# Six of the eight adaLN row tiles of a type, in the first norm's first half, loaded two at a time into the weights' hi and lo buffers

## The chip, the cores and the metric

The kernel runs on one core of a Trainium2 chip. The metric is the device time of one execution in microseconds, as the median over several runs; one execution was also taken with the hardware profiler. In what follows PE is TensorE's matmul side, PEld its weight loads, DVE is VectorE, ACT is ScalarE, POOL is GpSimd and SP is SyncE, which issues nearly all DMAs.

## The reference, cut to what matters

Two trunk layers of a diffusion backbone, in float32. Each sub-layer normalises its input and modulates it with a shift and a scale that come from a small vector `c` (for the 256 latent tokens) or `c_ctx` (for the 256 context tokens) through one large weight, `w_ada`. The change touches only the first such product of layer 0, so this is what must be seen:

```python
def rmsnorm(x, g):
    y = x * lax.rsqrt(jnp.mean(x * x, axis=-1, keepdims=True) + EPS)
    return y * g

def modulate(x, g, shift, scale):
    return rmsnorm(x, g) * (1 + scale) + shift

def adaln(v, w, b):                      # w: (1024, 6144)
    m = jax.nn.silu(v) @ w + b
    return jnp.split(m, 6, axis=-1)      # sh1, sc1, g1, sh2, sc2, g2

# layer l:
h  = modulate(x,  norm1[l], sh1, sc1)    # then h @ w_in and three token mixers, merge, MLP
hc = modulate(xc, norm1[l], csh1, csc1)
```

No column of the first norm's output can be formed before the shift and the scale of that column are there, and no matmul with `w_in` before that.

## The kernel before, in words

**Precision.** Every float32 product is made of three matmuls: an operand is split into a high part (ACT copies it to the rounded type `fp32r`) and a low part (DVE subtracts the high part from the operand). A weight tile of 128 x 1024 floats (512 KB) is loaded into a stage buffer `st` (4 buffers) and split into `wh` and `wl` (4 buffers each, `W_HL_BUFS`).

**The first norm's modulation.** Shift (type 0) and scale (type 1) of the first norm in layer 0 are computed as rows on PE. The 1024 columns of a type fall into two halves of 512 columns; for each half the class `First` accumulates, over the eight blocks `kk` of 128 rows of `w_ada`, a 4 x 512 product with the silu of `c` and `c_ctx` (two vectors, each with its hi and lo part). One block of one type and one half is a "row tile" of 128 x 512 floats, 256 KB. `ada_row` takes one of the 64 general buffers `b` for it and issues its load (`ad<-in_wada_dram` in the profile). `ada_use` splits it: ACT writes `ah` (a cast), DVE writes `al` (a subtraction), and `First.row` issues two matmuls (`ada<-ah,s` and `ada<-al,s`). After the eighth block `First.end` copies the 4 x 512 result out with ACT (`arow`), turns it into columns with matmuls (`adat`), and DVE adds the bias (`mod`); with both types there, DVE forms the factor `A`. Then ACT writes the first `hh`, the hi part of the normalised and modulated input, and the first matmul with `w_in` (`qkv<-wh,hh`) can start. The input itself comes in four tiles of 512 KB (`x` 0 and 1 latent, 2 and 3 context): ACT squares and sums them (`junk`), DVE and POOL make `rstd` (POOL's part is a power), DVE scales (`xh`), PE transposes (`xT`).

**What sets the order.** The list `START` gives the order of the first loads on SP's queue: tile (type 0, kk 0), `x` 0, `x` 1, the other 15 row tiles of half 0 with the types in turn, then the first weight tiles of `w_in` (`win`), `x` 2, one more `win`, the row tiles of half 1 with `x` 3 between them, and so on. Everything behind that, on every engine, is put in order while the program is written: each piece of work is a Python generator, and the scheduler `_Flow` runs the one of highest priority whose inputs are there by its own estimate of times (`fl.ready`, `fl.room` for buffers). A change of the estimated times early on can so change the written order later. `fl.room("w", ...)` is the count of `wh`/`wl` buffers in use, `fl.free` gives a buffer back.

```python
START = (
    [("ada", 0, 0, 0), ("x", 0), ("x", 1)]
    + [("ada", 0, typ, kk) for kk in range(KD) for typ in range(2)][1:]
    + [("win", 0, 0), ("win", 0, 1), ("x", 2), ("win", 0, 2)]
    + [("ada", 1, typ, kk) for kk in range(4) for typ in range(2)]
```

Of the kernel before, what the change touches and what calls it, by code (L numbers as in the profile page):

```python
# [8 lines left out]
F32 = mybir.dt.float32  # L9
F32R = mybir.dt.float32r  # L10
# [5 lines left out]
P = 128  # L16
D = 1024
KD = D // P
# [11 lines left out]
W_HL_BUFS = 4  # L30
# [30 lines left out]


START = (
    [("ada", 0, 0, 0), ("x", 0), ("x", 1)]
    + [("ada", 0, typ, kk) for kk in range(KD) for typ in range(2)][1:]
    + [("win", 0, 0), ("win", 0, 1), ("x", 2), ("win", 0, 2)]
    + [("ada", 1, typ, kk) for kk in range(4) for typ in range(2)]
    + [("x", 3)]
# [108 lines left out]
class _Flow:  # L177
# [58 lines left out]
    def free(self, *aps):  # L236

        for name in {ap.tensor.name for ap in aps}:
            self.shares[name] -= 1
            if self.shares[name]:  # L240
                continue
            p = self.pools[self.owner.pop(name)]
            p[0] -= 1
            p[1].append(self.uses[name] + 0.1)
# [48 lines left out]
P_NORM, P_ATT, P_SPLIT, P_SIDE, P_ADA, P_MAIN = range(6)  # L293
# [3 lines left out]
def kernel(ctx: ExitStack, tc: tile.TileContext, a: dict, out: bass.AP):  # L297
    nc = tc.nc
    ctx.enter_context(tc.manual_schedule())
    fl = _Flow()  # L300
# [6 lines left out]
    wp = ctx.enter_context(tc.tile_pool(name="wp", bufs=W_STAGE_BUFS))  # L307
# [6 lines left out]
    def nm(s):  # L314
        uid[0] += 1
        return f"{s}_{uid[0]}"

    def big(dt=F32, s="b"):
        t = bp.tile([P, 512], dt, tag="b", name=nm(s))
        fl.take("b", t)  # L320
        return t

    tmp = big
    free = fl.free
# [20 lines left out]
    def load(dst, src, queue=nc.sync):  # L345
        size = 4
        for d in dst.shape:
            size *= d
        fl.loaded(dst, size) if dst.space == bass.MemoryType.SB else None
        queue.dma_start(out=dst, in_=src)  # L350


    def stage(src, nk, ncol):

        yield from fl.room("st", 1, W_STAGE_BUFS)
        st = wp.tile([P, 1024], F32, tag="st", name=nm("st"))
        fl.take("st", st)
        v = st[:, : nk * ncol].rearrange("p (k n) -> p k n", k=nk)
        load(v, src)
        return v  # L360
# [8 lines left out]
    def halves(v, nk, ncol):  # L369

        yield fl.ready(v)
        yield from fl.room("w", 1, W_HL_BUFS)
        hi = wp.tile([P, 1024], F32R, tag="wh", name=nm("wh"), bufs=W_HL_BUFS)
        lo = wp.tile([P, 1024], F32R, tag="wl", name=nm("wl"), bufs=W_HL_BUFS)
        fl.take("w", hi)
        hv = hi[:, : nk * ncol].rearrange("p (k n) -> p k n", k=nk)
        lv = lo[:, : nk * ncol].rearrange("p (k n) -> p k n", k=nk)
        S.copy(out=hv, in_=v)
        yield fl.ready(hv)
        V.tensor_tensor(out=lv, in0=v, in1=hv.bitcast(F32), op=ALU.subtract)  # L380
        free(v)
        return hi, [(hv[:, k], lv[:, k]) for k in range(nk)]
# [56 lines left out]
    def mm3(ps, lh, rh, start, stop):  # L439

        PE.matmul(ps, lh[0], rh[0], start=start, stop=False)
        PE.matmul(ps, lh[0], rh[1], start=False, stop=False)
        PE.matmul(ps, lh[1], rh[0], start=False, stop=stop)
# [27 lines left out]
    x = [[None, None] for _ in range(NT)]  # L471
# [256 lines left out]
    def constants():  # L728
        load(rope, a["rope"])
        load(gains, a["gains"].to_broadcast([P, DEPTH, 4, HD]))  # L730
        load(sink, a["sink"].to_broadcast([P, DEPTH, NH]))
        load(icnt, a["icnt"])
        load(pscale, a["pscale"])
        fl.spawn(constants_use(), P_SIDE)
# [58 lines left out]
    def norm(l, which, stream, hT):  # L793
        xh = [[None, None, (_Event(), _Event())] for _ in range(2)]
        for i in range(2):
            fl.spawn(norm_tile(l, which, 2 * stream + i, xh[i]), P_NORM)
        first = (l, which) == (0, 0)
        if not first:
            yield ab_ev[l, which, stream][1]
        for k2 in range(0, KD, 2):  # L800
            for i in range(2):
                if late(xh[i][2][k2 // 4]):
                    yield xh[i][2][k2 // 4]
            if first and k2 == 4:
                yield ab_ev[l, which, stream][1]
            yield from banks()
            ps = bank("xT")
            for kk in range(2):
                k = k2 + kk
                for i in range(2):  # L810
                    c = (k % 4) * P
                    PE.transpose(ps[:, kk * 256 + i * P : kk * 256 + (i + 1) * P], xh[i][k // 4][:, c : c + P], ident)
            if k2 % 4 == 2:
                free(*[xh[i][k2 // 4] for i in range(2)])
            left = [0, 1]
            cols = slice(stream * 256, stream * 256 + 256)
            for kk in range(2):
                k = k2 + kk
                fl.spawn(mod_out(l, which, hT, stream, k, ps[:, kk * 256 : (kk + 1) * 256], cols, hT.ev[stream][k], H32_DVE.get((l, which, stream), ()), ps, left), P_NORM)
            yield  # L820
# [1166 lines left out]
    def main():  # L1987
        nxt = []

        def hT_next():  # L1990
            if not nxt:
                nxt.append(Normed())
            return nxt[0]

        yield from layer(0, h0, hT_next)
        yield from layer(1, nxt[0], None)
# [5 lines left out]
    def start():  # L2002

        def ada_row(half, typ, kk):
            yield from fl.room("b", 1, B_BUFS)
            raw = big(s="ad")
            load(raw, a["wada"][0, 2 * typ + half, kk // 4, :, kk % 4])
            fl.spawn(ada_use(first[half], typ, kk, raw), P_NORM)

        def ada_use(f, typ, kk, raw):  # L2010
            yield fl.ready(raw)
            yield from fl.room("b", 2, B_BUFS)
            hi, lo = big(F32R, "ah0"), big(F32R, "al0")
            S.copy(out=hi, in_=raw)
            yield fl.ready(hi)
            V.tensor_tensor(out=lo, in0=raw, in1=hi.bitcast(F32), op=ALU.subtract)
            free(raw)
            yield from f.row(typ, kk, (hi, lo))
            free(hi, lo)

        def x_rows(t):
            src = (a["x"] if t < 2 else a["ctx"])[0, t % 2 * P : t % 2 * P + P]
            v = yield from stage(src.unsqueeze(1), 1, D)
            for n in range(2):
                x[t][n] = v[:, 0, n * 512 : n * 512 + 512]
                fl.set(x_ev[t][n], v)
            if t % 2:
                fl.spawn(norm(0, 0, t // 2, h0), P_NORM)

        def win(kh, c):  # L2030
            if c < 2:
                k0, nk, ncol = 4 * kh + 2 * c, 2, 512
                src = a["win2"][0, 0]
            else:
                k0, nk, ncol = 4 * kh, 4, 256
                src = a["win"][0, CHUNKS[0][c]]
            v = yield from stage(src[:, k0 : k0 + nk], nk, ncol)
            fl.spawn(win_use(kh, c, v, nk, ncol), P_NORM)

        def win_use(kh, c, v, nk, ncol):  # L2040
            p, done = first_w[kh, c]
            p.extend((yield from halves(v, nk, ncol)))
            fl.set(done, *[q for r in p[1] for q in r])

        def mask_load():
            v = yield from stage(a["mask"], 2, P)
            fl.spawn(mask_use(v), P_NORM)

        def mask_use(v):
            yield fl.ready(v)  # L2050
            S.copy(out=mask, in_=v)
            free(v)

        first = [First(0), First(1)]
        fl.spawn(main(), P_MAIN)
        for it in START:
            if it[0] == "x":
                yield from x_rows(it[1])
            elif it[0] == "ada":
                yield from ada_row(*it[1:])  # L2060
            elif it[0] == "win":
                yield from win(*it[1:])
            elif it[0] == "const":
                constants()
            else:
                yield from mask_load()
        fl.spawn(ws.loads(), P_NORM)
        fl.spawn(ws.splits(), P_SPLIT)
        yield ab_ev[0, 0, 1][1]
        fl.set(layer_started[0])  # L2070

    plan_layer(0)
    plan_layer(1)
    fl.spawn(start(), P_NORM)
    fl.spawn(ada_all(), P_ADA)
    for l in range(DEPTH):
# [66 lines left out]
```

## Time and profile before

| | us |
|---|---|
| median of 3 runs | 1147.7 (1146.86 to 1148.02) |
| profiled execution, its own time | 1147.47 |
| its span, first to last instruction | 1145.7 |
| PE busy | 1123.3 (98%) |
| PEld busy | 946.2 (83%) |
| DVE busy | 890.5 (78%) |
| ACT busy | 646.9 (56%) |

The span is what the trace covers; 1.77 us of the profiled execution's own time lie outside it. A busy PE is not a PE at its peak, since matmuls are pipelined and their ends are modelled. DMA share is the mean busy share of the core's 16 DMA engines; for short stretches it can read a little over 1, because a packet counts where it begins.

### The profile page before, as it was taken

To read this page: it belongs to the slowest core of one execution; us is meant where nothing else is said; L and a number is where in the kernel's file an instruction comes from. 1 tells how busy PE (TensorE), PEld (TensorE's weight loads), DVE (VectorE), ACT (ScalarE), POOL (GpSimd) and SP (SyncE) were. 2 spreads that over 40 slices of the span, in tenths; PEclk is the share of its full clock that TensorE was granted. 3 is DMA by queue.
4 is the path that set the end of the run, shared out by engine and by line. 5 is a ranking of instruction groups with operands and counts; after the bars stand their busy time and mean duration, and the time that the engine had idled before them with its cause. 6 is when DMAs were issued, how large, how long until landed. Compare 5 with 4: busy or idle time off the path is not lost.

```text
span 1145.7 us, 16194 instructions
## 1 busy us (share of the span) xinstructions
PE 1123.3 (98%) x5760; PEld 946.2 (83%) x5760; DVE 890.5 (78%) x1681; ACT 646.9 (56%) x1372; POOL 64.2 (6%) x78
## 2 busy tenths in 40 slices
PE   6999999999999999999999999999999999999998
PEld 2788888888888898888888888889888888888886
DVE  6889888899899679888676734579777885999453
ACT  7867668657653574422133333576878864666432
POOL 1133002000000100000000000013010000000000
PEclk9999999999999999999999999999999999999999
DMA  9742332343554335455655533555325570776662
GB/s 333 268 151 92 119 124 80 114 163 120 166 170 158 123 120 195 155 194 174 200 202 187 200 112 106 171 166 176 104 69 171 178 264 1 247 261 209 191 213 75
DMA packets 59761, 186.74 MB, mean 163 GB/s; under 512 B 7040, under 2 KB 7824, under 8 KB 59680
## 3 DMA queue, kind: packets, MB, share of 16 engines
q1 hardware_dynamic: 59472, 185.63, 48.7%
q8 instruction: 45, 0.74, 0.3%
q14 instruction: 36, 0.29, 0.1%
q0 software_dynamic: 64, 0.07, 0.0%
q10 hardware_dynamic: 144, 0.01, 0.0%
HBM read 184.63 MB, written 1.05 MB: 162 GB/s over the span
## 4 chain that ended last, share of the span: by engine, by line
PE 89%; DVE 4%; ACT 4%; DMA 2%; issue 1%; SPq 0%; POOL 0%; DVEq 0%; ACTq 0%
PE tm L170 27%; PE h L170 22%; PE g L170 16%; PE qkv L170 6%; PE br L170 4%; PE po L170 2%; PE sc L170 2%; PE pT L174 2%; PE u L170 1%; DMA ad<-in_wada_dram 1%; ACT hh L136 1%; ACT p L136 1%; PE xT L174 1%; PE ada L170 1%; PE qT L174 1%
## 5 line engine op out<-in xcount | busy, mean ns | idle before, releaser
L136 DVE TENSOR_TENSOR wl<-st,wh 128x1024 fp32r<-128x1024 f32 x216 | 263.4, 1221 | 117.7 <-ACT wh L136 117.5
L136 ACT CAST wh<-st 128x1024 fp32r<-128x1024 f32 x216 | 227.9, 1059 | 224.2 <-PE tm L170 137.3
L170 PE MATMUL h<-hh,wh 128*128 128x512 f32 (+1 forms) x512 | 183.7, 378 | 0.0
L170 PE MATMUL h<-hh,wl 128*128 128x256 f32 (+1 forms) x512 | 168.2, 328 | 0.9 <-DVE wl L136 0.9
L136 DVE SCALAR_TENSOR_TENSOR acc<-sta,s_col,acc 128x512 f32<-128x512 f32 x224 | 159.3, 745 | 1.5 <-DMA sta<-in_wada_dram 1.1
L170 PE MATMUL tm<-wh,ah 128*128 128x512 f32 x384 | 149.9, 390 | 0.0
L170 PE MATMUL tm<-wl,ah 128*128 128x512 f32 x384 | 149.5, 389 | 0.0
L170 PE MATMUL tm<-wh,al 128*128 128x512 f32 x384 | 149.4, 389 | 0.0
L170 PEld LDWEIGHTS h<-hh,wh 128*128 128x128 f32 x512 | 96.2, 188 | 17.7
L170 PE MATMUL h<-hl,wh 128*128 128x512 f32 (+1 forms) x288 | 105.5, 366 | 0.1
L170 PEld LDWEIGHTS h<-hh,wl 128*128 128x128 f32 x512 | 96.6, 189 | 10.0 <-DVE wl L136 1.1
L170 PEld LDWEIGHTS tm<-wh,al 128*128 128x128 f32 x384 | 72.1, 188 | 15.2
L170 PEld LDWEIGHTS tm<-wl,ah 128*128 128x128 f32 x384 | 72.1, 188 | 14.9
L170 PEld LDWEIGHTS tm<-wh,ah 128*128 128x128 f32 x384 | 72.1, 188 | 14.6
L170 PE MATMUL g<-hh,wh 128*128 128x512 f32 x192 | 76.7, 400 | 0.0
L170 PE MATMUL g<-hh,wl 128*128 128x512 f32 x192 | 75.0, 391 | 0.0
L170 PE MATMUL g<-hl,wh 128*128 128x512 f32 x192 | 75.0, 391 | 0.0
L170 PE MATMUL qkv<-wh,hh 128*128 128x256 f32 (+1 forms) x192 | 66.1, 344 | 1.1 <-ACT hh L136 1.1
L170 PE MATMUL qkv<-wl,hh 128*128 128x256 f32 (+1 forms) x192 | 64.7, 337 | 1.8 <-DVE wl L136 1.8
L170 PE MATMUL qkv<-wh,hl 128*128 128x256 f32 (+1 forms) x192 | 64.8, 337 | 0.0
L170 PEld LDWEIGHTS h<-hl,wh 128*128 128x128 f32 x288 | 54.3, 189 | 9.2 <-DVE hl L136 0.5
L136 DVE TENSOR_REDUCE mx<-sc 128x1 f32<-128x512 f32 (+1 forms) x60 | 39.8, 685 | 20.8 <-PE sc L170 20.6
(213 smaller groups left out, 2238.0 us busy)
## 6 DMA issues: line engine op xcount, KB each, us to landing
st<-in_w_dram SPq DMA_DIRECT2D x136, 512.0 KB, 4.4
sta<-in_wada_dram SPq DMA_DIRECT2D x80, 512.0 KB, 4.1
st<-in_win_dram SPq DMA_DIRECT2D x48, 512.0 KB, 4.3
st<-in_wing_dram SPq DMA_DIRECT2D x24, 512.0 KB, 4.4
ad<-in_wada_dram SPq DMA_DIRECT2D x32, 256.0 KB, 6.7
st<-in_wout_dram SPq DMA_DIRECT2D x8, 512.0 KB, 4.5
wor<-in_wout_dram SPq DMA_DIRECT2D x16, 256.0 KB, 6.0
grow<-in_b_ada_dram SPq DMA_DIRECT2D x12, 256.0 KB, 5.5
```

Of the source, the lines that this page charges most:

```text
L136: return fn(*args, **kw)
L170: return self._e.matmul(out, lhsT, rhs, start=start, stop=stop)
L174: return self._e.transpose(out, in_, identity)
```

## The change

Blocks 0 to 5 of half 0 no longer come one row tile at a time. A new generator `ada_rows2(half, kk)` takes one pair of the `wh`/`wl` buffers and loads two consecutive blocks of type 0 into the first and the same two blocks of type 1 into the second: two loads of 512 KB in place of four of 256 KB. In `w_ada` as it lies in memory the two blocks of a row are next to each other, so that a partition's row is 4 KB long where it was 2 KB. Blocks 6 and 7 still come one by one. The uses are unchanged (`ada_use` for each of the four 512-column parts, in the order block, type), but the pair of buffers goes back only when all four are done. `x` 0 and `x` 1 now stand behind the first two loads, which hold four row tiles, where they stood behind one row tile.

```diff
 START = (
-    [("ada", 0, 0, 0), ("x", 0), ("x", 1)]
-    + [("ada", 0, typ, kk) for kk in range(KD) for typ in range(2)][1:]
+    [("ada2", 0, 0), ("x", 0), ("x", 1), ("ada2", 0, 2), ("ada2", 0, 4)]
+    + [("ada", 0, typ, kk) for kk in (6, 7) for typ in range(2)]
     + [("win", 0, 0), ("win", 0, 1), ("x", 2), ("win", 0, 2)]
     + [("ada", 1, typ, kk) for kk in range(4) for typ in range(2)]
     + [("x", 3)]
...
-        def ada_use(f, typ, kk, raw):
+        def ada_rows2(half, kk):
+
+            yield from fl.room("w", 1, W_HL_BUFS)
+            raws = [wp.tile([P, 1024], F32R, tag=t, name=nm(t), bufs=W_HL_BUFS) for t in ("wh", "wl")]
+            fl.take("w", raws[0])
+            left = [4]
+            for typ in range(2):
+                v = raws[typ].bitcast(F32).rearrange("p (k n) -> p k n", k=2)
+                load(v, a["wada"][0, 2 * typ + half, kk // 4, :, kk % 4 : kk % 4 + 2])
+            for k in range(2):
+                for typ in range(2):
+                    v = raws[typ].bitcast(F32)[:, k * 512 : k * 512 + 512]
+                    fl.spawn(ada_use(first[half], typ, kk + k, v, raws[0], left), P_NORM)
+
+        def ada_use(f, typ, kk, raw, both=None, left=None):
             yield fl.ready(raw)
             yield from fl.room("b", 2, B_BUFS)
             hi, lo = big(F32R, "ah0"), big(F32R, "al0")
             S.copy(out=hi, in_=raw)
             yield fl.ready(hi)
             V.tensor_tensor(out=lo, in0=raw, in1=hi.bitcast(F32), op=ALU.subtract)
-            free(raw)
+            if both is None:
+                free(raw)
+            else:
+                left[0] -= 1
+                if not left[0]:
+                    free(both)
             yield from f.row(typ, kk, (hi, lo))
             free(hi, lo)
...
+            elif it[0] == "ada2":
+                yield from ada_rows2(*it[1:])
```

## Rows read from the trace of the kernel before

**Rows 1.** The page: span, and busy time by engine.

```profile
span 1145.7 us, 16194 instructions
PE 1123.3 (98%) x5760; PEld 946.2 (83%) x5760; DVE 890.5 (78%) x1681; ACT 646.9 (56%) x1372; POOL 64.2 (6%) x78
```

**Rows 2.** Stretches: length, busy by engine (count), granted clock, DMA share, GB/s.

```profile
0.00:25.20 25.20, 14.17 (x56) 5.83 (x56) 15.19 (x33) 17.89 (x36) 4.58 (x14) 0.98 0.94 326
25.20:60.00 34.80, 34.80 (x180) 26.02 (x181) 29.22 (x66) 27.88 (x56) 4.49 (x2) 0.92 0.73 261
```

**Rows 3.** Waits of PE from 25.3 us on: total, times, longest; ten groups, 7.9 us.

```profile
PE qkv L170 <- DVE wl L136: 1.8, 1, 1.8
```

**Rows 4.** The chain of work that ended last, from 0 us: start, length, what.

```profile
11.79 6.69 DMA ad<-in_wada_dram
...
22.42 0.58 ACT arow L136
...
25.20 7.11 PE qkv L170 x18
```

**Rows 5.** Timeline of ACT from 12 us: start, length, instruction, count, idle before it.

```profile
17.17 3.33 ACT L136 CAST ah<-ad 128x512 fp32r<-128x512 f32 x5 [0.29 <-DMA ad<-in_wada_dram]
20.99 0.58 ACT L136 COPY arow<-ada 4x512 f32<-4x512 f32 x1 [0.49 <-PE ada L170]
21.47 1.04 ACT L136 CAST wh<-st 128x1024 fp32r<-128x1024 f32 x1
```

**Rows 6.** Timeline of DVE from 6 us, columns as in rows 5.

```profile
12.15 0.88 DVE L136 TENSOR_SCALAR xh<-st,rstd 128x512 f32<-128x512 f32 x2 [0.45 <-POOL rstd L136]
12.95 3.69 DVE L136 TENSOR_TENSOR al<-ad,ah 128x512 fp32r<-128x512 f32 x6
...
17.82 3.40 DVE L136 TENSOR_TENSOR al<-ad,ah 128x512 fp32r<-128x512 f32 x5 [0.22 <-ACT ah L136]
```

**Rows 7.** DMA traffic from 24 to 28 us, nearly all in 2 KB packets.

```profile
DMA packets 835, 1.53 MB, mean 383 GB/s; under 512 B 93, under 2 KB 93, under 8 KB 835
```

**Rows 8.** DMA traffic from 20 to 22 us, all in 4 KB packets.

```profile
DMA packets 237, 0.84 MB, mean 422 GB/s; under 512 B 31, under 2 KB 31, under 8 KB 237
```

**Rows 9.** Stretches of the first loads, columns as in rows 2.

```profile
8.00:12.00 4.00, 2.17 (x6) 0.48 (x6) 2.95 (x8) 3.60 (x9) 1.98 (x2) 1.00 1.05 369
12.00:16.00 4.00, 4.00 (x19) 2.32 (x17) 3.85 (x8) 2.89 (x5) 0.12 (x1) 1.00 0.99 307
```

**Rows 10.** Timeline of SP: start, length, issues, count.

```profile
2.12 12.02 SPq L350 DMA_DIRECT2D ad<-in_wada_dram  x15
...
16.32 0.33 SPq L350 DMA_DIRECT2D st<-in_ctx_dram  x1
17.22 0.33 SPq L350 DMA_DIRECT2D st<-in_win_dram  x1
```

**Rows 11.** Timeline of POOL: the powers of the second and the third input tile.

```profile
10.58 1.53 POOL L136 TENSOR_TENSOR rstd<-rstd,neg_half 128x1 f32<-128x1 f32 x1 [1.73 <-DVE rstd L136]
...
33.99 3.94 POOL L136 TENSOR_TENSOR rstd<-rstd,neg_half 128x1 f32<-128x1 f32 x1 [21.88 <-DVE rstd L136]
```

**Rows 12.** Timeline of PE: matmuls of the row tiles and the transposes.

```profile
11.72 0.63 PE L170 MATMUL ada<-ah,s 128*4 128x512 f32 x1
12.15 0.63 PE L170 MATMUL ada<-al,s 128*4 128x512 f32 x1
...
12.58 1.70 PE L174 MATMUL xT<-ident,xh 128*128 128x128 f32 x8
...
14.59 0.40 PE L170 MATMUL ada<-ah,s 128*4 128x512 f32 x1
14.82 0.39 PE L170 MATMUL ada<-al,s 128*4 128x512 f32 x1
```

**Rows 13.** Stretches around the start of layer 1, columns as in rows 2.

```profile
771.00:774.00 3.00, 3.00 (x19) 3.00 (x18) 3.00 (x10) 2.96 (x10) 2.12 (x1) 0.61 0.57 172
774.00:777.00 3.00, 3.00 (x23) 3.00 (x22) 3.00 (x9) 0.37 (x4) 1.16 (x2) 0.82 0.84 242
```

## The prediction, made before the changed kernel was run

> **What bounds the kernel now.** I read first the page: PE is busy 98% of a span of 1145.7 us, the next engine 78% [rows 1]. So a change in the first 25 us is worth what it moves the point from which PE runs without a break. The table of stretches shows where that point lies: up to 25.20 us PE is busy 14.17 us, from there to 60 us all of 34.80 [rows 2]. The list of PE's waits behind that point has ten groups that sum to 7.9 us, the longest a single one of 1.8 us [rows 3]. I call the start of the first `qkv` matmul at 25.20 us T0; a shift of T0 goes through to the end nearly one for one.
>
> What sets T0 is in the chain of waits [rows 4]: a load of a row tile issued at 11.79 that lands 6.69 later, at 18.48, the split and matmuls of the last tiles, the second `arow` copy at 22.42, then `adat`, `mod`, `A`, the first `hh`, and `qkv` at 25.20. From `arow`'s start to T0 it is 2.78 us, and the change touches nothing in that part. So the sum ends with: when does the second `arow` start? The timelines of ACT and DVE show the steps before it [rows 5, 6]. The last five casts take 3.33 us, one per (3.33 - 0.62) / 4 = 0.68 us, which is the pace at which tiles land, since ACT waited for a DMA before them. DVE follows at the same pace: five `al` in 3.40 us, ended at 21.22. When DVE has a backlog it is faster: six in 3.69, so (3.69 - 0.69) / 5 = 0.60 us each. Before the change DVE waits for tiles at the end, then; it has a reserve of only 0.08 us a tile.
>
> **Part by part: the loads.** Sixteen loads of 256 KB become six of 512 KB and four of 256 KB. The bytes ahead of the last row tile are the same, 16 x 256 KB and 2 x 512 KB of `x`, and the DMA engines have no gap in them: share 1.05 and 0.99 in the two stretches of four microseconds where most of these tiles come [rows 9]. SP's 15 issues spread over 12.02 us [rows 10] because it waits for earlier landings (the 11.79 load is issued as an earlier one lands), not because issuing is slow. So only the speed of the bytes counts. 2 KB packets move 383 GB/s from 24 to 28 us (742 packets over 512 B in 1.53 MB, 2.06 KB each) [rows 7]; 4 KB packets move 422 from 20 to 22 us (206 in 0.84 MB) [rows 8]. The twelve merged tiles hold 3.15 MB: 8.2 us at the one rate, 7.5 at the other, 0.7 us gained. The lower bound is 0 (the difference comes from the time, not the packet). The upper: over 8 to 16 us the rate was (369 + 307) / 2 = 338 [rows 9]; if 4 KB packets cured all of that, 9.3 - 7.5 = 1.8 us. I take 0.6, near the first pair, since in 24 to 28 us the same 2 KB packets did much better than 338, so the slow stretch isn't due to their size.
>
> **The burst.** Tiles now land in pairs of a type, and that costs. The eighth 512 KB load carries the last merged blocks; before, the same 4096 KB had landed when the twelfth cast began at 17.17 (the first of the last five). With 0.6 gained it lands at 16.55. Behind it are six `al`: two of its own blocks, four of blocks 6 and 7. Cast 0.62, a hand-over of 0.03, five `al` at 0.60, the last 0.69: 16.55 + 0.65 + 3.00 + 0.69 = 20.9, against 21.22 before. So DVE is the bound now, and of 0.6 us gained in landing 0.3 is left. With nothing gained it is 21.5, 0.3 late. With 1.8 gained, 19.7 by this line, but DVE must have done what is before it: about 17.1, by the next paragraph, and six more are 17.1 + 3.69 = 20.8, 0.4 early.
>
> **The input tiles move back.** 768 KB more lie ahead of `x` 0 and 1, at 369 GB/s 2.1 us [rows 9]. The second tile's `xh` ran at 12.15 to 13.03 behind POOL's power [rows 6]; now I put it at 13.3 to 14.2. DVE loses nothing by that in sum: the four `al` of the first pair fill its first microseconds instead. But from 14.2 it has five `al` to do before those of the eighth load, 5 x 0.60 = 3.0, free at about 17.1, just when the first of the six is ready (16.55 + 0.65 = 17.2). So there is no slack left. POOL's power is a risk here: it took 1.53 us for the second tile and 3.94 for the third [rows 11], both times beside `al`, and `xh` waits for it in DVE's queue with the `al` behind it. The Trainium skill ("GPSIMD Engine Reference", section 1, Specifications) says that POOL shares SBUF interfaces with VectorE and contends with VectorE instructions of two SBUF inputs; `al` is one, the rows agree, and by it the power could be held for as long as an `al` is in front of `xh`. I expect one `al` there; one more costs 0.6 us of DVE.
>
> **What is hidden.** `xT` needs `xh`, but its reader is the first `hh`, just ahead of T0, so 1.2 us more is covered by the ten microseconds between. SP's queue: the load of `x` 2 needs the buffer of `x` 0 and the third `win` that of `x` 1; they were issued at 16.32 and 17.22 [rows 10], and `xh` gives up the second of the buffers at 14.2 and the first sooner, so neither waits longer than now, nor do the half 1 loads behind them. The `wh`/`wl` pairs: three of four are taken, the first `win` split gets the fourth and the second the one that the first pair of blocks leaves, the earliest of all, while these splits begin at 21.47 [rows 5] and later. Twelve fewer `b` buffers cost nothing. Earlier landing of `win` and half 1 gains nothing, as PE has no gap behind T0 [rows 2].
>
> **Sum.** `al` ends 0.3 earlier. The second `arow` stands in ACT's queue behind the first and the 1.04 us `wh` cast [rows 5]; that cast starts when the first `arow` is through, not at its data, so the shift of the last but one `al` passes on: 0.2 to 0.3. If the written order puts the `wh` cast ahead of both `arow`, the two `adat` groups stand back to back and the shift is near 0. I take T0 0.2 us earlier: 1147.47 (the profiled execution's own time) - 0.2 = 1147.3; the median of the runs is 0.2 above that execution, so 1147.5 for the median. The direct bounds are T0 from 0.4 earlier to 0.9 later (0.3 for no gain and 0.6 for the power).
>
> **Rivals.** (1) *The loads' count was the bound*, each one carrying a price of its own: landings come so early that DVE alone sets the end. From 8 to 16 us DVE idles 1.05 + 0.15 us [rows 9], and the last five `al` lose 4 x 0.08 and the 0.22 ahead of them [rows 6]; with landings never late these 1.7 us are what can be won, 1145.8 by the profiled execution's own time, 1146.0 as a median. Against it: 256 KB tiles land 0.68 apart at the end, and 256 KB at 383 GB/s are 0.68, which leaves nothing for a fixed price. The Trainium skill ("DMA: Bandwidth & Descriptors", Rules for kernel authors, and the Anatomy of one DMA for POOL's path) says to coalesce transfers and gives a fixed cost of about 2 us a DMA; by that, paid one after the other, six fewer would be an estimated 12 us of loading. By that rule too DVE would set the end. (2) *PE at half clock.* Around 11.72 matmuls of 512 columns start 0.43 us apart, the 1.2 GHz level, at 14.59 0.23 apart, the 2.4 one; the clock column reads 1.00 in both, but the spacing decides [rows 9, 12]. Ahead of the rise stand matmuls and eight transposes without a break [rows 12]. Now PE has less to do from 10 to 13 us, and the transposes come at 14.2. At half clock a tile's two matmuls take 0.86, more than DVE's 0.60. After T0 the mean of 0.92 over 34.8 us [rows 2] means 0.08 x 34.8 / 0.5 = 5.6 us at half clock, under matmuls without a break; the same from 14.2 gives 19.8. By then PE has done 1.7 us of transposes and 3.9 / 0.86, four and a half tiles; six and a half at 0.46 end at 22.8, so the second `arow` starts 0.4 to 0.6 us behind the 22.42 of before [rows 4]: 1148.2 as a median. (3) *Slower: the written order.* The scheduler's estimates move by tenths, and work behind can be put otherwise. The place that shows the price is the start of layer 1: PE waited 1.8 us there for one `wl` [rows 3], and right after the granted clock fell to a mean of 0.61 and 0.82 for three microseconds each [rows 13], 3 x 0.39 + 3 x 0.18 = 1.7 us of full speed. A second such place costs 3.5: 1147.7 + 3.5 = 1151.2. It decides once such a `wl` is some 1.5 us late and the clock falls behind it. For it: the order is sensitive; against it: only one place in 1120 us is like that. (4) *Faster by the same*: that wait goes, and the clock holds: 1147.5 - 3.5 = 1144.0.
>
> **Chances.** The forecast with its bounds 0.58; (1) 0.08; (2) 0.10; (3) 0.11; (4) 0.13. A measurement of this kernel can tell about 0.2%, 2.3 us, from no change: forecast, (1) and (2) lie within it, 0.76; faster 0.13, slower 0.11. The range reaches from 1145.0, below (1) and part of the way to (4), to 1150.0, above (2) and part of the way to (3): some 0.8.
>
> **What would show it.** Landing: the cast of block 6, type 0 begins at 17.2 to 18; no difference from 17.8 would make the gain 0. Burst: the last six `al` run 0.60 apart, with no wait for ACT between them, ending at 20.7 to 21.1. Order: `xh` of `x` 1 behind one `al`, at about 13.3. Clock: matmuls of row tiles 0.23 apart from 17 us on. T0 at 24.8 to 25.3, and a list of PE's waits behind it that sums to 8 us as now. The prediction is wrong if that list or the clock in the later stretches changes by over 2 us, or if PE, not DVE, is late before T0.

## The result, and the profile after

The changed kernel takes 1160.49 us (median of 4 runs, 1159.28 to 1162.35) against 1147.86 for the kernel before on the same chip (4 runs, 1146.86 to 1148.57): a ratio of 1.0114 [1.0102, 1.0125], 12.6 us slower. The profiled execution took 1162.35 us, with a span of 1160.3; that of before is 1145.7 [rows 1]. The two profiles differ by 14.6 us, a little more than the medians. The number of PE's instructions is the same, and PE is busy 5.7 us longer (1123.3 before [rows 1]); the other 8.9 us are PE idle.

The page of the kernel after, span and busy time by engine:

```profile
span 1160.3 us, 16202 instructions
PE 1129.0 (97%) x5760; PEld 950.2 (82%) x5760; DVE 891.3 (77%) x1681; ACT 645.4 (56%) x1372; POOL 66.8 (6%) x78
```

To see where the time went, both spans are cut at the same five pieces of PE's work: the first `qkv` (T0), the first matmul of the gates `g` in layer 0's attention, the first `h` of layer 0's MLP, the first `qkv` of layer 1, and shortly before the last `h` of its MLP. Stretches of the kernel before, columns as in rows 2 (its first stretch stands there):

```profile
25.20:85.00 59.80, 59.80 (x313) 47.66 (x314) 49.44 (x140) 44.80 (x159) 14.84 (x19) 0.95 0.64 223
85.00:393.10 308.10, 307.15 (x1575) 259.65 (x1574) 270.25 (x553) 192.34 (x444) 21.59 (x18) 1.00 0.40 130
393.10:752.90 359.80, 358.75 (x1701) 300.85 (x1701) 260.27 (x373) 144.42 (x206) 3.80 (x4) 1.00 0.49 166
752.90:1053.40 300.50, 295.61 (x1732) 259.77 (x1731) 250.39 (x536) 215.35 (x499) 19.44 (x24) 0.99 0.51 167
1053.40:1145.70 92.30, 87.85 (x389) 72.41 (x387) 44.95 (x49) 32.07 (x34) 0.00 (x0) 0.99 0.51 164
```

The same pieces of work in the kernel after:

```profile
0.00:25.50 25.50, 14.05 (x57) 6.17 (x57) 14.78 (x33) 17.47 (x38) 4.02 (x14) 0.92 0.93 346
25.50:86.50 61.00, 59.95 (x312) 47.93 (x313) 52.13 (x132) 39.53 (x128) 7.72 (x12) 0.95 0.63 218
86.50:404.30 317.80, 311.05 (x1576) 262.07 (x1575) 272.93 (x569) 196.86 (x472) 29.59 (x25) 0.99 0.38 126
404.30:764.10 359.80, 358.73 (x1702) 300.87 (x1701) 256.02 (x365) 144.41 (x206) 3.80 (x4) 1.00 0.49 165
764.10:1068.20 304.10, 297.40 (x1733) 260.86 (x1732) 250.57 (x537) 215.16 (x499) 21.67 (x24) 0.99 0.50 165
1068.20:1160.30 92.10, 87.78 (x389) 72.34 (x387) 44.88 (x49) 32.01 (x34) 0.00 (x0) 0.99 0.50 164
```

The `h` are the matmuls of an MLP's first product. Line by line the differences are 0.3, 1.2, 9.7, 0.0, 3.6 and -0.2 us: 14.6. The change touches the first stretch, and that lost 0.3. Two thirds were lost in layer 0's attention, 60 us and more behind the last instruction that the change edits. There PE idles 317.80 - 311.05 = 6.75 us where it idled 0.95, and it is busy 3.9 longer with the same work.

The DVE column offers a reason why this stretch is the tender one: DVE is busy 270.25 of 308.10 us in it, 88%, where layer 0's MLP has 72%; that MLP got a new order too and lost nothing. But the reason is not shown. Layer 1's stretch of the kernel before, cut at the first `h` of its MLP, reads:

```profile
752.90:961.20 208.30, 204.32 (x1173) 178.10 (x1172) 168.38 (x383) 155.33 (x386) 18.88 (x23) 0.99 0.46 149
961.20:1053.40 92.20, 91.29 (x560) 81.67 (x559) 82.01 (x153) 60.02 (x113) 0.56 (x1) 1.00 0.63 207
```

The 3.6 us were lost in the first part, with DVE at 81%. The second part has DVE at 89% and lost nothing; but there every engine kept its order, so it is no test.

PE's waits behind T0 in the kernel after, columns as in rows 3 (the 1.8 is the one of rows 3). `pm` is the product of the pooling mixer, of `ph` and `pl`, the high and low parts of `pooled`; `po` is attention's product of the transposed probabilities (`pth`, `ptl`) with the values:

```profile
PE pm L170 <- ACT ph L136: 3.7, 1, 3.7
PE po L170 <- DVE ptl L136: 3.0, 3, 1.4
PE qkv L170 <- DVE wl L136: 1.8, 1, 1.8
PE po L170 <- DVE t L136: 1.4, 1, 1.4
```

The longest, in PE's timeline:

```profile
109.79 0.49 PE L170 MATMUL pm<-ph,wph 128*128 128x512 f32 x1 [3.67 <-ACT ph L136]
111.31 0.79 PE L170 MATMUL pm<-pl,wph 128*128 128x512 f32 x1 [1.03 <-DVE pl L136]
...
112.33 0.63 PE L170 MATMUL g<-hh,wh 128*128 128x512 f32 x1
112.75 0.63 PE L170 MATMUL g<-hl,wh 128*128 128x512 f32 x1
```

And the stretches at it, columns as in rows 2:

```profile
106.00:110.40 4.40, 0.61 (x2) 0.19 (x1) 4.34 (x13) 1.78 (x5) 1.31 (x2) 1.00 0.65 177
110.40:117.20 6.80, 5.89 (x14) 4.64 (x15) 6.41 (x14) 2.60 (x4) 4.48 (x2) 0.50 0.12 46
```

One place thus costs twice: 3.67 + 1.03 us of waiting, and from 110.4 on 6.8 us at a granted clock of 0.50, the 1.2 GHz level, in which the `g` matmuls start 0.43 us apart. PE is busy for 5.89 of these 6.8 us, so the clock costs 5.89 x 0.5 = 2.9 us more (the rest of the stretch is idle that the waits already count). The releaser is `ph` on ACT, but ACT had stood idle. What `ph` waited for is in DVE's timeline:

```profile
104.47 1.22 DVE L136 TENSOR_TENSOR wl<-st,wh 128x1024 fp32r<-128x1024 f32 x1
...
106.07 0.69 DVE L136 TENSOR_TENSOR ach<-acc,ach 64x512 fp32r<-64x512 f32 x1
106.79 1.23 DVE L136 TENSOR_TENSOR wl<-st,wh 128x1024 fp32r<-128x1024 f32 x1
107.93 0.48 DVE L136 TENSOR_TENSOR y<-qkv,gains 128x128 f32<-128x128 f32 x2
108.33 0.75 DVE L136 TENSOR_TENSOR pooled<-pooled,upad 128x256 f32<-128x256 f32 x2
```

and ACT's:

```profile
109.12 0.62 ACT L136 CAST ph<-pooled 128x512 fp32r<-128x512 f32 x1 [0.36 <-DVE pooled L136]
```

DVE is full (4.34 of 4.40 us) with work of other chains, two weight splits and the gate's `ach` among it, written ahead of the `pooled` that PE's next matmul hangs on. Nothing there is slower than before (a `wl` split takes 1.22 us in both); it stands in another order. In the kernel before PE came to the same product at 107.31 and did not wait, since DVE had begun `pl` at 106.03:

```profile
106.03 0.68 DVE L136 TENSOR_TENSOR pl<-pooled,ph 128x512 fp32r<-128x512 f32 x1
...
107.31 0.40 PE L170 MATMUL pm<-ph,wph 128*128 128x512 f32 x1
```

The 3.6 us of layer 1's attention are of the same kind: `po` waits 1.35 at 832.40 and 1.41 at 834.19, and 3.4 us at 0.50 follow.

### The profile page after: what moved, and what is told of

Read it like the earlier page. It is cut to its first block, busy times and chain, and to the rows that moved or that the text cites. A ratio compares the mean times of both kernels' runs of the same rounds, so it can differ in the third digit from the quotient of the medians.

```text
span 1160.3 us, 16202 instructions
## 1 busy us (share of the span) xinstructions
PE 1129.0 (97%) x5760; PEld 950.2 (82%) x5760; DVE 891.3 (77%) x1681; ACT 645.4 (56%) x1372; POOL 66.8 (6%) x78
## 3 DMA queue, kind: packets, MB, share of 16 engines
HBM read 184.63 MB, written 1.05 MB: 160 GB/s over the span
## 4 chain that ended last, share of the span: by engine, by line
PE 86%; ACT 6%; DVE 5%; issue 1%; DMA 1%; POOL 0%; SPq 0%; DVEq 0%; ACTq 0%; POOLq 0%
PE tm L170 28%; PE h L170 22%; PE g L170 15%; PE br L170 5%; PE qkv L170 5%; PE po L170 2%; PE sc L170 2%; PE pT L174 2%; ACT p L136 1%; PE ada L170 1%; ACT hh L136 1%; DVE wl L136 1%; ACT wh L136 1%; ACT sq L136 1%; ACT h L136 1%
## 5 line engine op out<-in xcount | busy, mean ns | idle before, releaser
L136 DVE TENSOR_REDUCE mx<-sc 128x1 f32<-128x512 f32 (+1 forms) x60 | 40.0, 685 | 17.2 <-PE sc L170 17.0
```

What stands on the lines that cost most here:

```text
L136: return fn(*args, **kw)
```

## The experiments

Ratios are against the kernel before on the same chip, with the 95% interval. Every kernel here computes all of the reference. Theory: the loads cost nothing, the order of the instructions behind them does. Rival: the loads (their landing, the burst, T0) cost, and the order is an onlooker.

**1. The loads without the order.** `START` is that of before. The 512 KB loads and their buffers are real, but the scheduler is told of 256 KB tiles, so that every engine but SP keeps the order of before.

```diff
         def ada_row(half, typ, kk):
+            if half == 0 and kk < 6:
+                if typ == 0 and kk % 2 == 0:
+                    for ty in range(2):
...
+                        nc.sync.dma_start(out=duos[ty, kk].rearrange("p (k n) -> p k n", k=2), in_=...)
+                raw = duos[typ, kk - kk % 2][:, kk % 2 * 512 : kk % 2 * 512 + 512]
+                fl.loaded(raw, 4 * P * 512)
```

> The loads of the changed kernel, in its order on SP and into its buffers, but the order of every other instruction as in the kernel before (the scheduler is told of sixteen loads of 256 KB). If the written order is the cause: 1147 to 1149 us, and no wait of over 2 us for the pooling product at 110 us. If the loads, their buffers or the later input tiles are the cause: 1157 to 1161 us.

Measured: 1147.9 us, ratio 1.0003 [0.9993, 1.0012]. In the traces PE, DVE, ACT and POOL run the same sequence as in the kernel before, instruction for instruction. So the loads alone are worth nothing, to within 0.12%. Its stretches up to layer 0's MLP, columns as in rows 2:

```profile
0.00:26.40 26.40, 14.05 (x57) 5.63 (x57) 14.75 (x33) 16.77 (x36) 4.59 (x14) 1.00 0.94 350
26.40:85.10 58.70, 58.70 (x312) 46.60 (x313) 49.81 (x141) 45.05 (x160) 12.56 (x19) 0.97 0.62 210
85.10:393.30 308.20, 307.25 (x1575) 259.69 (x1574) 269.83 (x552) 191.97 (x443) 21.58 (x17) 1.00 0.40 130
```

T0 is 1.2 us later than before, and at the first `g` 0.1 is left of it. PE has no gap in either kernel between the two points; the clock gave it back: 0.97 over 58.7 us against 0.95 over 59.8 before, 59.8 x 0.05 - 58.7 x 0.03 = 1.2. So a later T0 needn't arrive at the end.

**2. The order without the loads.** `START` and the scheduler's picture are those of the change, but sixteen loads of 256 KB are issued, in the order of before.

```diff
         def ada_rows2(half, kk):
...
+                fl.loaded(v, 4 * P * 1024)
+                todo.extend((k, typ, kk, v) for k in range(2))
+            todo.sort(key=lambda q: (q[2] + q[0], q[1]))
+            while todo:
+                k, typ, k0, v = todo.pop(0)
+                nc.sync.dma_start(out=v[:, k], in_=a["wada"][0, 2 * typ + half, (k0 + k) // 4, :, (k0 + k) % 4])
```

> The loads of the kernel before, sixteen of 256 KB in the old order on SP, but every other instruction in the order of the changed kernel. If the written order is the cause: 1158 to 1162 us, with the wait for the pooling product and the half clock behind it. If the loads are the cause: 1147 to 1149 us.

Measured: 1160.29 us, 1.0109 [1.0091, 1.0127], the whole loss without one merged load; on the four engines it runs the sequence of the kernel after, instruction for instruction. With run 1 the rival is out.

**3 and 4. Which part of the change turns the order?** Run 3 only moves `x` 0 and 1 behind four single row tiles; run 4 merges the loads and leaves `x` as early as it can stand, behind the first of them.

```diff
-    [("ada", 0, 0, 0), ("x", 0), ("x", 1)]
-    + [("ada", 0, typ, kk) for kk in range(KD) for typ in range(2)][1:]
+    [("ada", 0, typ, kk) for kk in range(2) for typ in range(2)]
+    + [("x", 0), ("x", 1)]
+    + [("ada", 0, typ, kk) for kk in range(2, KD) for typ in range(2)]
```

> All row tiles loaded singly as before; only the two input tiles move from behind the first row tile to behind the fourth. If the scheduler's estimates are what flips the order, and the place of the input tiles is enough for that: 1157 to 1162 us without any merged load. If the merged loads are needed: 1147 to 1149 us.

> Merged loads as in the change, but the input tiles right behind the first 512 KB load, the scheduler free to order. If the place of the input tiles alone flipped the order: 1147 to 1149 us. If any of the change's two parts flips it: 1157 to 1162 us. If the loads themselves cost: 1157 or more as well, which the first two runs tell apart.

Measured: 1161.48, 1.0115 [1.01, 1.013], and 1159.31, 1.0098 [1.0083, 1.0113]. Either part alone is enough; neither is the culprit. Both tip the program into one and the same order: from 17 us on, the four engines run the sequence of the kernel after in both. So the kernel after and runs 2 to 4 are one order with four sets of loads, and lie within 2.2 us. In runs 2 to 4 the same `pm` waits as in the kernel after, 3.34, 3.11 and 2.80 us.

**5 and 6. One group of instructions as the cause.** `acc`, the sums of layer 0's first gate on DVE, is through with all eight blocks at 75.3 us in the kernel after, seven of them ahead of the norms of q and k; in the kernel before three are done at 63.6, and the fourth runs at 100.58. Run 5 is the kernel after with `acc` held at the fourth block about as long; run 6 the kernel before with `acc` let go.

```diff
+                if (l, j, kk) == (0, 4, 3):
+                    while fl.now < HOLD:
+                        yield HOLD
                 yield from V.calm(ADA_CALM[l])
```

```diff
-                yield from V.calm(ADA_CALM[l])
+                if (l, j) != (0, 4):
+                    yield from V.calm(ADA_CALM[l])
```

> The changed kernel, with one thing held: the adaLN accumulation of layer 0's first gate (DVE's acc) stops ahead of its fourth block until 93.5 us of the scheduler's own time, as it did in the kernel before, in place of running ahead of the q and k norms. If these acc, queued on DVE ahead of the norms, are the main cost: the wait for the pooling product at 110 us and the half clock behind it go, 1149 to 1153 us. If the loss is spread over the whole new order: 1157 to 1161 us.

> The kernel before, loads and order, but the acc of layer 0's first gate no longer wait until DVE's queue is short, so that all eight blocks run by 80 us. If acc ahead of the norms are the main cost: PE waits for the pooling product or for q and k at 100 to 115 us, 1152 to 1159 us. If not: 1147 to 1149 us.

Measured: 1159.08, 1.0103 [1.0088, 1.0118], and 1165.36, 1.0148 [1.0131, 1.0165]. Letting `acc` go is enough to do harm, more than was expected: in run 6 PE waits 3.72 us for `pl` at 106.17, then 2.46 at 197.35 and 2.36 at 258.95. But holding it doesn't cure. In run 5 the wait at 110 us is gone, and another stands 140 us later; its PE timeline and the stretch behind:

```profile
252.09 0.38 PE L171 MATMUL po<-pth,v 128*128 128x256 f32 x1 [3.21 <-ACT pth L137]
253.89 0.58 PE L171 MATMUL po<-ptl,v 128*128 128x256 f32 x1 [1.42 <-DVE ptl L137]
```

```profile
253.30:260.10 6.80, 6.21 (x23) 5.73 (x24) 5.24 (x9) 0.97 (x3) 0.00 (x0) 0.50 0.19 70
```

The theory that one misplaced group carries the loss fell. What was tested next is whether it is this order at all, or any order but the one before.

**7 to 11. Other orders of both kernels.** The scheduler reckons a DMA's bytes at 360e3 a microsecond. This constant touches no load and no work, only the estimated times and so the order.

```diff
-        self.dma = max(self.dma, self.queue + 0.65) + nbytes / 360e3
+        self.dma = max(self.dma, self.queue + 0.65) + nbytes / 385e3
```

"Pairs" is the changed kernel, "single" the one before; in the last three the constant is 359e3 or 365e3.

> The changed kernel, with one number of the scheduler's estimate changed: its DMA rate is 385 GB/s in place of 360 (the trace has 383). If the written order is the cause and the estimate tips it: 1146 to 1150 us, with qkv taken up again at about 46 us as in the kernel before. If the merged loads cost by themselves: 1157 or more.

> The kernel before with the same one number, 385 in place of 360; from some 20 us on its order is that of the run with merged loads at 385. If the merged loads are worth nothing by themselves: within 1 us of that run. If landing 2 us earlier is worth its time: that run is 1 to 2 us faster than this one.

> The kernel before with one constant of the scheduler's estimate of a DMA's time changed by 0.3% (360e3 to 359e3 bytes a microsecond): the loads, their order, the buffers and the work are those of before; what is queued next on some engines differs. Theory (the order that happens to be written decides, and the order of before is a good one among its neighbours): if the order in layer 0's attention stays, 1147 to 1149; if it tips, 1156 to 1165, by one or two waits of PE of 2 to 4 us there and half clock right behind. Rival (only the later or earlier T0 tips the order, a constant that moves the early estimates by under 0.1 us doesn't): 1147 to 1149.

> The same constant by 1.4% (365e3). Theory: the order tips as in the five orders of this study that cost 11 to 18 us, so 1155 to 1165, with a wait of PE over 2 us in layer 0's attention, not at the place of the changed kernel in particular. Rival (it is the estimate of a fuller first stretch in the changed kernel that hurts, not any shift): within 3 us of 1148.

> The changed kernel with the same constant of 365e3. Theory: the loads cost nothing, so that an order with no long wait of PE in layer 0 would give 1146 to 1149; whether this constant gives one is open, with most of the weight on 1155 to 1165, since six of seven orders so far were of that kind. Rival (something in the paired loads themselves costs): over 1155 whatever the list of PE's waits says.

| loads, constant | us | ratio | first `h` of layer 0's MLP at, us (before 393.1) | PE's waits of over 1.5 us in layer 0's attention |
|---|---|---|---|---|
| single, 359e3 | 1151.02 | 1.0042 [1.0027, 1.0057] | 391.9 | none |
| single, 365e3 | 1157.52 | 1.0101 [1.008, 1.0122] | 403.0 | 4.21 at 191.57 |
| single, 385e3 | 1161.0 | 1.0123 [1.0108, 1.0138] | 406.5 | 4.22 at 192.55, 1.95 at 261.89 |
| pairs, 360e3 (the change) | 1160.49 | 1.0114 [1.0102, 1.0125] | 404.3 | 3.67 at 109.79 |
| pairs, 365e3 | 1150.44 | 1.003 [1.0018, 1.0041] | 394.9 | none |
| pairs, 385e3 | 1160.58 | 1.0114 [1.0099, 1.0129] | 406.6 | 4.22 at 192.71, 1.95 at 262.05 |

Three of the five were not as the theory expected. "Pairs, 385e3" did not come back to 1146 to 1150 but fell into the range named for loads that cost by themselves; "single, 385e3", which from 20 us on runs the same sequence without a merged load, takes as long. "Single, 359e3" and "pairs, 365e3" lie between the two ranges named for each, a little above the lower one.

The kernel before loses 0.42% by a constant changed by 0.3%, and 1.0% by 1.4%. The changed kernel gets 9 of its 12.6 us back by the same 1.4%, with its loads as they are.

The 4 us of "single, 359e3" lie elsewhere: the four engines keep the order of before up to 314 us, layer 0's attention loses nothing, and layer 1's attention takes 213.5 us (751.7 to 965.2) against 208.3. In its PE timeline, with the stretch at it:

```profile
820.09 0.39 PE L170 MATMUL po<-pth,v 128*128 128x256 f32 x1 [1.35 <-DVE t L136]
821.88 0.58 PE L170 MATMUL po<-ptl,v 128*128 128x256 f32 x1 [1.41 <-DVE ptl L136]
```

```profile
821.00:827.80 6.80, 5.92 (x21) 5.42 (x22) 4.50 (x9) 4.43 (x8) 0.00 (x0) 0.50 0.24 77
```

In PE's timeline of "single, 365e3", the wait that cost it most:

```profile
191.57 0.79 PE L170 MATMUL g<-hh,wl 128*128 128x512 f32 x1 [4.21 <-DVE wl L136]
```

At the first `g` that kernel had been 1.7 us ahead of the one before (83.3 against 85.0). In "pairs, 365e3" PE's waits behind T0 and the stretch of layer 0's attention read:

```profile
PE po L170 <- DVE ptl L136: 1.9, 3, 0.9
PE qkv L170 <- DVE wl L136: 1.8, 1, 1.8
...
PE tm L170 <- DVE yh L136: 1.0, 1, 1.0
```

```profile
84.90:394.90 310.00, 307.56 (x1576) 259.77 (x1575) 267.18 (x545) 193.11 (x442) 18.84 (x16) 1.00 0.38 126
```

The longest wait in that stretch is the 1.0 of `tm` (the `qkv` of 1.8 is that of rows 3, in layer 1), the clock holds at 1.00, and it is 1.9 us longer than before instead of 9.7. (Its profiled execution took 1148.6, less than its median.) No kernel here beats the one before.

## Why the prediction was wrong

Forecast: no change, 1147.5 us, range 1145.0 to 1150.0. Measured: 1160.49, slower.

**The step that failed** is rival (3), the written order, in its chance and in its size. The sum has no term for it: it takes all work behind T0 as unchanged. The rival got 0.11, on the ground that "only one place in 1120 us is like that". But the scarcity of such places in the trace of before tells of one order; it says nothing of the orders next to it. Of the seven orders tried besides that of before (the kernel after and runs 2 to 4 share one, the two kernels at 385e3 another), none was as quick, two cost about 4 us and the rest 11 to 18. The price was off as well: one place at 3.5 us, from the 1.8 us wait and the clock behind it [rows 3, 13]. The place at 110 us cost 3.67 + 1.03 + 2.9 = 7.6, and there were more. PE's waits behind T0 sum to 16.4 us where the prediction, which named this as a sign of being wrong, had 8. What rows 1 and 2 did show, and the prediction passed over, is that DVE is the next limit; by stage it is 88% in layer 0's attention, where every wait of over 2 us lies that a new order brought.

**The sum's first sentence**, that a shift of T0 goes to the end nearly one for one, does not hold as a rule. In run 1 the +1.2 us at T0 were 0.1 at the first `g`. In the new order a shift did go through: run 2's T0 is 27.12 against 25.50 in the kernel after, 1.6 later, and its span 1161.7 against 1160.3. There the clock over the 61 us up to the first `g` is 0.95 in both; in run 1 it was 0.97 against 0.95.

**Loads.** Taken 0.6 us earlier, bounds 0 and 1.8. By the DMA records the last row tile landed at 17.76 us, 19.85 before: 2.1 earlier, past the upper bound; the cast of block 6, type 0, began at 16.64, ahead of the forecast 17.2 to 18. The rate over 8 to 16 us rose from 338 [rows 9] to (409 + 396) / 2 = 402 GB/s. This pair of traces lies at the upper end: the six kernels with merged loads have 17.7 to 18.6 us and 384 to 407 GB/s, the seven with single ones 18.5 to 19.9 us and 338 to 377. Stretches of the kernel after, the last one for the clock:

```profile
8.00:12.00 4.00, 3.56 (x8) 0.76 (x8) 3.00 (x7) 4.00 (x12) 0.56 (x1) 1.00 1.03 409
12.00:16.00 4.00, 2.34 (x11) 1.61 (x12) 3.45 (x9) 3.52 (x8) 0.97 (x1) 0.85 1.03 396
14.80:18.20 3.40, 3.40 (x13) 1.78 (x12) 3.40 (x7) 3.13 (x7) 0.00 (x0) 0.50 1.05 402
```

The prediction took the small gain because the 2 KB packets of 24 to 28 us had done better than 338 [rows 7]; with 4 KB packets in their place the slow stretch was gone. Whether the longer rows or the smaller number of loads does it was not told apart. The fixed cost of about 2 us a DMA that the Trainium skill gives for POOL's path ("DMA: Bandwidth & Descriptors", Anatomy of one DMA), from which the prediction reckoned an estimated 12 us of loading, does not show here as one paid load after load; 2.1 us is what came.

**Burst.** Right: the last six `al` run 0.60 us apart with no wait for ACT. But they end at 21.52, outside the forecast 20.7 to 21.1. In DVE's timeline of the kernel after:

```profile
8.02 1.29 DVE L136 TENSOR_TENSOR al<-wh,ah 128x512 fp32r<-128x512 f32 x2 [0.94 <-ACT ah L136]
...
14.82 0.68 DVE L136 TENSOR_TENSOR al<-wh,ah 128x512 fp32r<-128x512 f32 x1
...
19.03 2.49 DVE L136 TENSOR_TENSOR al<-ad,ah 128x512 fp32r<-128x512 f32 x4
```

From 14.82 to 21.52 stand eleven `al` without a break. DVE began them too late, for a reason that the prediction missed: the first `al` ran at 8.02, 6.74 before. ACT, whose first cast stood behind the silu, waited for the silu's input `s_raw` until 5.98; the first tile was there at 5.81. The chain of waits of the kernel after shows it at its start, and PE at its end:

```profile
0.74 5.24 DMA s_raw<-in_cc_dram
...
13.02 0.98 POOL rstd L136
14.02 0.50 DVE xh L136
...
14.56 1.56 PE xT L174 x7
16.12 5.67 PE ada L170 x20
21.81 0.58 ACT arow L136
...
25.50 7.43 PE qkv L170 x18
```

`s_raw`, 8 KB on ACT's queue, landed at 5.98, 4.69 before.

**Input tiles.** Right in order: `xh` of `x` 1 behind one `al`. It came at 14.02 instead of 13.3; the late start fits these 0.7 us, since the chain runs through both. POOL's power took 0.97 us beside that `al`, and 0.56 for `x` 0 with no `al` beside it; there the trace agrees with the rule of the Trainium skill ("GPSIMD Engine Reference", section 1, Specifications).

**Rival (2), PE at half clock**, came true: 14.8 to 18.2 us at 0.50, and from 15.77 on PE ran the row tiles without a break, the last `al` matmul at 21.84. So PE, not DVE, was last ahead of T0 in the chain, the prediction's other sign of being wrong. The price did not come as told: the half clock lasted 3.4 us, not 5.6, and the second `arow` started at about 22.3, 0.1 earlier than before, not 0.4 to 0.6 later. T0 came at 25.50, 0.3 later where the forecast had 0.2 earlier and the bounds +0.9: from that `arow` to T0 it was 3.2 us, where the prediction held 2.78 fixed. With the `wh` cast ahead of both `arow`, all 16 `adat` matmuls stood back to back, a case that the sum had named. Rival (1) is out: DVE and PE set the end, but T0 did not come sooner. **What is hidden** held for SP's queue, which is not in the chain, but not for `xT`: the chain runs from POOL's power for `x` 1 over `xh` and `xT` to the row tiles' matmuls. Behind T0, "no gap" didn't hold: 1.05 us of idle PE up to 86.5 us, in two waits for DVE's `h` at 49 and 50 us.

What stays open: why a given order gets its long wait where it does. The scheduler puts an instruction where its inputs are ready by its own estimate, so that at such a place the estimate should be ahead of the chip; by how much, and in which of its costs, was not measured.

## What to carry to other kernels

Where a program puts its instructions in order from estimated times, price a change in two parts: the edit itself, and a draw of a new order. Look at the stages whose order moves and in which the second engine is nearly full, however far from the edit: here the one with DVE at 88% took every wait of over 2 us. That is a place to look first, not a rule; one order lost its 4 us in a stage with DVE at 81%. And separate the two on the chip by running the new transfers in the old order and the old transfers in the new one; here the kernel before had the quickest of eight orders, so the change, which brought the first order that came, was not compared with it on equal terms.

## What the runs showed of the hardware

- PE idle of 4.6 to 4.7 us in two pieces, close together, came with 6.8 us at the granted clock of 0.50, from within the second piece on (at 110.4 after, at 253.3 in run 5); in the kernel after, with PE busy for 5.89 of them, this cost 2.9 us more. Two waits of 1.4 us close together came with 3.4 us of it at 834 after, and 6.8 at 821 in "single, 359e3": the same two waits, and not the same price.
- A small transfer on ACT's queue (8 KB, `s_raw`) landed 1.3 us later when the first load on SP's queue was of 512 KB and not of 256 KB (5.98 against 4.69), and the first `al` came as much later. The six kernels whose first load is of 512 KB have 5.55 to 5.98, the seven others 3.78 to 4.77.
- Over 8 to 16 us the DMA engines moved 402 GB/s with row tiles of 4 KB rows, and 338 with those of 2 KB, the share being about 1 in both; over all kernels 384 to 407 against 338 to 377.
